# The last two eighths of both MLPs taken by halves of the tokens, with VectorE's queue pinned around them

## The chip, the cores and the metric

The program runs on one core of one Trainium2 chip. The metric is device time of one execution in microseconds (us); three runs of the kernel before took 1609.48, 1611.65 and 1611.97 us, so the median is 1611.65 us. TensorE (PE in the profile) multiplies matrices into PSUM, VectorE (DVE) and ScalarE (ACT) work on SBUF and PSUM, GpSimd (POOL) on SBUF, and SyncE (SP) issues the transfers. Each of these queues runs its instructions in order.

## The reference

Two transformer blocks on 512 tokens of width 1024. Both end in an MLP with a squared ReLU:

```python
# first block
h = rms_norm(x, norm_mlp[l])
x = x + jnp.square(jax.nn.relu(h @ w_up[l])) @ w_down[l]
return rms_norm(x, norm_final)
# second block
n2 = rms_norm_2(h, norm_mlp_pre[l])
hid = jnp.square(jax.nn.relu(jnp.einsum('bsd,df->bsf', n2, w_up[l])))
mlp_out = jnp.einsum('bsf,fd->bsd', hid, w_down[l])
h = h + rms_norm_2(mlp_out, norm_mlp_post[l])
```

The hidden width is 4096. What comes before the MLPs (block attention and gated linear attention, cross attention, the gated MLP of the second block and its dilated attention) is not touched.

## The kernel before

Products are made to float32 accuracy from three passes: each operand is split into a high part (ScalarE copies it to the narrower format) and a low part (VectorE subtracts the high part from the source). `split` (L316, L317) does this for activations, `load` (L247 to L249) for weights: a transfer into a staging tile `st` (three buffers), the copy on ScalarE, the subtraction on VectorE, after which the staging tile is free for a later transfer. `mm3` (L304) issues the three matmuls.

`mlp` holds the hidden layer as eight eighths `r[0]` to `r[7]`, each of 512 hidden columns by 512 tokens. `up(m)` makes 128 of those columns in a PSUM bank of the `tr` pool (two banks), and `evac` takes it out with a ReLU on ScalarE (L1033) and a square on GpSimd (L1034). The first six eighths go down in three rounds `g` of seven products `i`, in sums and differences of halves, as in Strassen's scheme. A product accumulates in two PSUM banks, one for each `c` in 0 and 1, and `fold` adds a bank to the output on VectorE (L1085) when the product is done. Products 0, 3, 5 and 6 share the banks named x: product 6 goes on accumulating in the bank that product 5 left, so its first matmul for a `c` has to wait until `fold` of product 5 has read that bank. After each product stands one `up`, after the seventh two.

The last two eighths, `e` = 6 and 7, go down plainly: for each token chunk `c` of 128 tokens and each half `b` of the output columns one bank with twelve matmuls (a unit, below). Eighth 6 goes first, `b` by `b`; then eighth 7, `c` by `c`, and `done(c, b)` starts what follows a finished chunk. In the first MLP that is `norm2` (L943 to L967: norms of the chunk on ScalarE, GpSimd and VectorE, then eight transposes on TensorE and the splits into `ah` and `al`); the second block's first products (`heads_qk` by `fm_halves`, tokens 0 to 255 first, then 256 to 511) wait for it. In the second MLP it is the final norm and the output.

The program's order on each queue comes from a scheduler that places each instruction where its own time model thinks it ready. Tile pools choose the buffer by the same model. `issue_after(ins)` queues what is traced inside it on the engine of `ins` behind `ins`, in order only.

Of the kernel before, what the change touches and what calls it, by code (L numbers as in the profile page):

```python
# [10 lines left out]
F32R = mybir.dt.float32r  # L11
# [9 lines left out]
P = 128  # L21
T = 512
D = 1024
KT = 8
NC = 4
# [85 lines left out]
class Kernel:  # L111
# [907 lines left out]
    def mlp(self, sfx, h, out, fresh, done):  # L1019

        nc, th = self.nc, self.th
        self.enter("pf" + sfx)
        key, up_key = f"w_down{sfx}", f"w_up{sfx}"
        r = {}

        def evac(m, ps):
            e = m // 4
            if m % 4 == 0:  # L1030
                r[e] = self.m8([P, 4, T], F32, "relu")
            t = r[e][:, m % 4, :]
            nc.scalar.activation(t, ps, AF.Relu)  # L1033
            nc.gpsimd.tensor_mul(t, t, t)  # L1034

        def up(m):
            (w,) = [self.weight(up_key, m, ahead=2)]
            ps = self.tr()
            for k in range(KT):
                self.mm3(ps, w[0][:, k, :], w[1][:, k, :], *self.a_all()(k), k == 0, k == KT - 1)  # L1040
            evac(m, ps)


        w = [self.weight(up_key, m, ahead=3) for m in range(4)]
        pss = [self.acc() for _ in range(4)]
        for hf in range(2):
            yield [h[2 * hf], h[2 * hf + 1]]
            s = slice(256 * hf, 256 * hf + 256)
            for i, p in enumerate(pss):
                for k in range(KT):  # L1050
                    self.mm3(p[:, s], w[i][0][:, k, :], w[i][1][:, k, :], *self.a_all(s)(k), k == 0, k == KT - 1)
                yield
        for m, ps in enumerate(pss):
            evac(m, ps)
        for m in range(4, 8):
            up(m)
            yield
        lo, hi = slice(0, 256), slice(256, 512)
        keep = {n: self.k4([P, 2, 512], F32, n) for n in ("p1", "p5", "u2")}
        sums = {}  # L1060

        def a_sum(g, i):

            a, b = r[2 * g], r[2 * g + 1]
            src = (a[:, :, lo], b[:, :, lo], None, None, None, a[:, :, lo], b[:, :, hi])[i]
            if i == 2:
                sums["t"] = src = self.ph.tile([P, 4, 256], F32, tag="asum", bufs=1, name=self.name("asum"))
                nc.gpsimd.tensor_add(src, a[:, :, hi], b[:, :, hi])
            elif i == 3:
                src = sums["t"]  # L1070
                nc.gpsimd.tensor_sub(src, src, a[:, :, lo])
            elif i == 4:
                src = sums["t"]
                nc.gpsimd.tensor_sub(src, b[:, :, lo], src)
            elif i == 5:
                nc.gpsimd.tensor_sub(src, src, a[:, :, hi])  # L1076
            t = self.m8([P, 2, 4, 256], F32R, "as")
            self.split(src, t[:, 0], t[:, 1])
            sums[g, i] = t

        def put(dst, ps, first):
            if first:
                nc.scalar.activation(dst, ps, AF.Copy)
            else:
                nc.vector.tensor_add(dst, dst, ps)  # L1085

        def fold(i, c, g):

            ps = sums["xyzxzxx"[i]][c]
            n = {0: "p1", 2: "p5", 3: "u2"}.get(i)  # L1090
            if n:
                put(keep[n][:, c, :], ps, g == 0)
            else:
                put(out(*{1: (c, 0), 4: (c, 1), 5: (2 + c, 1), 6: (2 + c, 0)}[i]), ps, g == 0 and fresh)

        for g in range(3):
            for i in range(7):
                for j in range(i, min(i + 3, 7)):
                    if (g, j) not in sums:
                        a_sum(g, j)  # L1100
                w = self.weight(key, g, i, ahead=2)
                ch = "xyzxzxx"[i]
                if i < 3:
                    sums[ch] = [(self.aux if i == 1 else self.acc)() for _ in range(2)]
                t = sums[g, i]
                for c in range(2):
                    for k in range(4):
                        wh, wl = (v[:, k % 2, :] for v in w[k // 2])
                        self.mm3(sums[ch][c], t[:, 0, k, self.cs(c)], t[:, 1, k, self.cs(c)], wh, wl,
                                 i < 3 and k == 0, k == 3, more=i >= 3)  # L1110
                    fold(i, c, g)
                    yield
                up(8 * g + 8 + i)
                yield
                if i == 6:
                    up(8 * g + 15)
                    yield
        for n, c0, b in (("p1", 0, 0), ("u2", 0, 1), ("p5", 2, 1)):
            for c in range(2):
                nc.gpsimd.tensor_add(out(c0 + c, b), out(c0 + c, b), keep[n][:, c, :])  # L1120

        for e in (6, 7):
            hl = [self.m8([P, 4, T], F32R, "hid") for _ in range(2)]
            for k in range(4):
                self.split(r[e][:, k, :], hl[0][:, k, :], hl[1][:, k, :])
            w = [None, None]
            for c, b in [(c, b) for c in range(NC) for b in range(2)] if e == 7 else [(c, b) for b in range(2) for c in range(NC)]:
                if c == 0:
                    w[b] = self.weight(key, 8 * b + e)
                ps = self.acc()  # L1130
                self.tm(ps, lambda k: (hl[0][:, k, self.cs(c)], hl[1][:, k, self.cs(c)]), [w[b]])
                put(out(c, b), ps, False)
                if e == 7:
                    done(c, b)
                yield


    def block2_mix(self):
# [492 lines left out]
```

## Time and profile before

| | us |
|---|---|
| median of three runs | 1611.65 |
| the profiled execution | 1610.89 |
| its span in the trace | 1609.1 |
| TensorE busy with matmuls | 1580.2 |
| VectorE, ScalarE, GpSimd busy | 971.2, 686.6, 531.0 |

The profiled execution is 0.76 us below the median. The span is what the trace covers; the remaining 1.8 us lie around it. Times in the trace count from the span's start. A row of the timeline has its start, how long it lasted, the engine, the line, the operation, what it writes and reads, its shape, a count when equal rows were merged, and in brackets the idle time of the engine before it with what ended that.

### The profile page before, as it was taken

To read this page: it belongs to the slowest core of one execution; us is meant where nothing else is said; L and a number is where in the kernel's file an instruction comes from. 1 tells how busy PE (TensorE), PEld (TensorE's weight loads), DVE (VectorE), ACT (ScalarE), POOL (GpSimd) and SP (SyncE) were. 2 spreads that over 40 slices of the span, in tenths; PEclk is the share of its full clock that TensorE was granted. 3 is DMA by queue.
4 is the path that set the end of the run, shared out by engine and by line. 5 is a ranking of instruction groups with operands and counts; after the bars stand their busy time and mean duration, and the time that the engine had idled before them with its cause. 6 is when DMAs were issued, how large, how long until landed. Compare 5 with 4: busy or idle time off the path is not lost.

```text
span 1609.1 us, 21890 instructions
## 1 busy us (share of the span) xinstructions
PE 1580.2 (98%) x8930; PEld 1342.8 (83%) x8930; DVE 971.2 (60%) x1195; ACT 686.6 (43%) x1053; POOL 531.0 (33%) x360
## 2 busy tenths in 40 slices
PE   9999999999999999999999999999999999999987
PEld 8777878898898888887799899888888988888876
DVE  5566575554657868686644554464245567686844
ACT  6455464343444534344523333374323445353431
POOL 1121220000017474762250532330021274756621
PEclk9999999999999999999999999999999999999999
DMA  8404223421341323223403302322424523232221
GB/s 289 157 28 138 90 75 114 156 79 53 98 157 61 132 91 118 90 82 133 140 27 136 101 21 86 105 79 85 164 80 157 191 71 131 90 119 81 88 94 66
DMA packets 50437, 171.08 MB, mean 106 GB/s; under 512 B 6208, under 2 KB 6992, under 8 KB 50336
## 3 DMA queue, kind: packets, MB, share of 16 engines
q1 hardware_dynamic: 50336, 169.68, 31.2%
q8 instruction: 70, 1.15, 0.3%
q14 instruction: 31, 0.25, 0.0%
HBM read 163.35 MB, written 8.93 MB: 107 GB/s over the span
## 4 chain that ended last, share of the span: by engine, by line
PE 44%; POOL 2%; DVE 2%; issue 1%; ACT 1%; DMA 0%; POOLq 0%; DVEq 0%; ACTq 0%
PE acc L304 34%; PE tr L304 7%; PE aux L304 2%; POOL raw L289 1%; PE tr L313 1%; DVE acc L1085 0%; DMA st<-in_w_down 0%; DVE as L317 0%; DVE acc L1507 0%; ACT junk L1495 0%; DVE wlo L249 0%; DVE wt L317 0%; POOL relu L1076 0%; DVE wu L249 0%; POOL relu L1034 0%
## 5 line engine op out<-in xcount | busy, mean ns | idle before, releaser
L304 PE MATMUL tr<-ah,wu 128*128 128x512 f32 x896 | 283.1, 389 | 0.0
L249 DVE TENSOR_TENSOR wlo<-st,whi 128x1024 fp32r<-128x1024 f32 (+3 forms) x159 | 200.6, 1286 | 125.0 <-ACT whi L248 100.2
L248 ACT ACTIVATE whi<-st 128x1024 fp32r<-128x1024 f32 (+3 forms) x159 | 160.9, 1039 | 196.9 <-PE acc L304 113.2
L304 PE MATMUL acc<-ah,whi 128*128 128x512 f32 (+1 forms) x576 | 213.1, 372 | 0.8 <-ACT ah L316 0.8
L304 PE MATMUL acc<-wt,as 128*128 128x512 f32 x864 | 205.3, 393 | 8.4 <-DVE acc L1085 4.8
L304 PE MATMUL acc<-al,whi 128*128 128x512 f32 (+1 forms) x576 | 212.2, 369 | 0.6 <-DVE al L317 0.6
L304 PE MATMUL acc<-ah,wlo 128*128 128x512 f32 (+1 forms) x576 | 211.6, 368 | 0.0
L317 DVE TENSOR_TENSOR wt<-raw,wt 128x1024 fp32r<-128x1024 f32 x84 | 169.8, 2036 | 54.8 <-ACT wt L316 47.0
L304 PEld LDWEIGHTS acc<-wt,as 128*128 128x128 f32 x864 | 164.1, 190 | 43.5 <-DVE acc L1085 5.2
L304 PEld LDWEIGHTS tr<-ah,wu 128*128 128x128 f32 x896 | 168.3, 188 | 35.0
L304 PE MATMUL tr<-al,wu 128*128 128x512 f32 x448 | 174.3, 389 | 0.0
L1034 POOL TENSOR_TENSOR relu<-relu 128x512 f32<-128x512 f32 x64 | 94.1, 1472 | 209.7 <-ACT relu L1033 182.9
L289 POOL TENSOR_TENSOR raw<-raw,raw 128x1024 f32<-128x1024 f32 x48 | 153.7, 3217 | 14.4 <-DMA raw<-in_w_down 9.6
L304 PE MATMUL acc<-whi,ah 128*128 128x512 f32 (+2 forms) x432 | 146.5, 346 | 1.4 <-ACT ah L434 1.4
L304 PE MATMUL acc<-wlo,ah 128*128 128x512 f32 (+2 forms) x432 | 146.1, 342 | 0.0
L304 PE MATMUL acc<-whi,al 128*128 128x512 f32 (+2 forms) x432 | 144.2, 342 | 0.0
L316 ACT ACTIVATE wt<-raw 128x1024 fp32r<-128x1024 f32 x84 | 87.9, 1055 | 89.0 <-POOL raw L289 58.7
L304 PEld LDWEIGHTS acc<-ah,whi 128*128 128x128 f32 x576 | 108.9, 190 | 19.7 <-issue 1.7
L304 PEld LDWEIGHTS acc<-ah,wlo 128*128 128x128 f32 x576 | 109.4, 190 | 17.8
L304 PEld LDWEIGHTS acc<-al,whi 128*128 128x128 f32 x576 | 109.5, 190 | 17.6 <-DVE al L317 0.8
L249 DVE TENSOR_TENSOR wu<-st,wu 128x1024 fp32r<-128x1024 f32 x64 | 107.7, 1690 | 25.2 <-ACT wu L248 25.2
L304 PEld LDWEIGHTS tr<-al,wu 128*128 128x128 f32 x448 | 84.1, 188 | 17.4
(344 smaller groups left out, 2801.8 us busy)
## 6 DMA issues: line engine op xcount, KB each, us to landing
st<-in_w_up SPq DMA_DIRECT2D x64, 512.0 KB, 4.2
raw<-in_w_down SPq DMA_DIRECT2D x48, 512.0 KB, 4.7
st<-in_w_in_2f SPq DMA_DIRECT2D x44, 512.0 KB, 4.3
st<-in_w_in_u SPq DMA_DIRECT2D x20, 512.0 KB, 5.1
st<-in_w_out SPq DMA_DIRECT2D x16, 512.0 KB, 4.3
st<-in_w_down SPq DMA_DIRECT2D x16, 512.0 KB, 3.8
st<-in_w_xk SPq DMA_DIRECT2D x8, 512.0 KB, 4.5
st<-in_w_xv SPq DMA_DIRECT2D x8, 512.0 KB, 4.0
```

What stands on the lines that cost most here:

```text
L248: nc.scalar.activation(hi[:, s, :], st, AF.Copy)
L249: nc.vector.tensor_sub(lo[:, s, :], st, f32(hi[:, s, :]))
L289: nc.gpsimd.tensor_sub(r[name][:, s, :], r[x][:, s, :], r[y][:, s, :])
L304: self.nc.tensor.matmul(ps, lhsT, rhs, start=start, stop=stop, skip_group_check=more)
L313: self.nc.tensor.transpose(ps, src, self.ident)
L316: self.nc.scalar.activation(hi, src, AF.Copy)
L317: self.nc.vector.tensor_sub(lo, src, f32(hi))
L1034: nc.gpsimd.tensor_mul(t, t, t)
```

## The change

`fold` keeps the instruction that adds the fifth-index product's last bank (`i == 5`, `c == 1`) to the output. In the third round, the weight that product 6 asks for ahead of its use and the last `up` are queued on VectorE behind that addition, and so are the splits of the operands of eighths 6 and 7. The sixteen units of those eighths are reordered: first eighth 6 with `b` = 0 for all four chunks (the first two of these in the `aux` banks instead of `acc`), then what is left of chunks 0 and 1, then what is left of chunks 2 and 3. So the new list goes by halves of the tokens.

```diff
-                nc.vector.tensor_add(dst, dst, ps)
+                self.folded = nc.vector.tensor_add(dst, dst, ps).ins
...
-                w = self.weight(key, g, i, ahead=2)
+                late = g == 2 and i == 6
+
+                with self.tc.issue_after(folded) if late else ExitStack():
+                    w = self.weight(key, g, i, ahead=2)
...
+                    if i == 5:
+                        folded = self.folded
...
-                    up(8 * g + 15)
+                    with self.tc.issue_after(folded) if late else ExitStack():
+                        up(8 * g + 15)
...
-        for e in (6, 7):
-            hl = [self.m8([P, 4, T], F32R, "hid") for _ in range(2)]
-            for k in range(4):
-                self.split(r[e][:, k, :], hl[0][:, k, :], hl[1][:, k, :])
-            w = [None, None]
-            for c, b in [(c, b) for c in range(NC) for b in range(2)] if e == 7 else [(c, b) for b in range(2) for c in range(NC)]:
...
+        hl, w = {}, {}
+        units = [(6, 0, c) for c in range(NC)]
+        units += [(e, b, c) for e, b in ((6, 1), (7, 0), (7, 1)) for c in range(2)]
+        units += [(6, 1, c) for c in (2, 3)] + [(7, b, c) for c in (2, 3) for b in range(2)]
+        for n, (e, b, c) in enumerate(units):
+            if e not in hl:
+                hl[e] = [self.m8([P, 4, T], F32R, "hid") for _ in range(2)]
+                with self.tc.issue_after(folded):
+                    for k in range(4):
+                        self.split(r[e][:, k, :], hl[e][0][:, k, :], hl[e][1][:, k, :])
...
+            ps = (self.aux if n < 2 else self.acc)()
```

Three places show how the queues move. The first is VectorE at the end of the third round in the first MLP. `x_3230` and `x_3232` are the output chunks 2 and 3, `acc_6048` and `acc_6049` the x banks for `c` = 0 and 1, `hid_6572` the low part of eighth 6, `wu_6460` the weight of the last `up`, `wlo_6492` and `wlo_6529` the down weights of eighth 6. Before:

```order
L249 TENSOR_TENSOR wu_6460<-st_6461,wu_6460 128x1024
L1085 TENSOR_TENSOR x_3226<-x_3226,acc_6196 128x512
L1085 TENSOR_TENSOR x_3228<-x_3228,acc_6197 128x512
L249 TENSOR_TENSOR wlo_6492<-st_6493,whi_6491 128x1024
L249 TENSOR_TENSOR wlo_6492<-st_6497,whi_6491 128x1024
L1085 TENSOR_TENSOR x_3230<-x_3230,acc_6048 128x512
L317 TENSOR_TENSOR hid_6572<-relu_6106,hid_6571 128x512 x2
L249 TENSOR_TENSOR wlo_6529<-st_6530,whi_6528 128x1024
L249 TENSOR_TENSOR wlo_6529<-st_6534,whi_6528 128x1024
L317 TENSOR_TENSOR hid_6572<-relu_6106,hid_6571 128x512 x2
L1085 TENSOR_TENSOR x_3232<-x_3232,acc_6049 128x512
```

The same place of the changed kernel:

```order
L1085 TENSOR_TENSOR x_3226<-x_3226,acc_6196 128x512
L1085 TENSOR_TENSOR x_3228<-x_3228,acc_6197 128x512
L249 TENSOR_TENSOR wlo_6492<-st_6493,whi_6491 128x1024
L249 TENSOR_TENSOR wlo_6492<-st_6497,whi_6491 128x1024
L1085 TENSOR_TENSOR x_3230<-x_3230,acc_6048 128x512
L1085 TENSOR_TENSOR x_3232<-x_3232,acc_6049 128x512
L249 TENSOR_TENSOR wu_6460<-st_6461,wu_6460 128x1024
L249 TENSOR_TENSOR wlo_6529<-st_6530,whi_6528 128x1024
L249 TENSOR_TENSOR wlo_6529<-st_6534,whi_6528 128x1024
L317 TENSOR_TENSOR hid_6572<-relu_6106,hid_6571 128x512 x4
```

The addition to `x_3232` has moved from behind six instructions to directly behind the one to `x_3230`; `wu_6460`, ahead of all of them before, now stands behind both. The second MLP shows the same two lists with other numbers.

The second place is ScalarE there; `relu_6391<-tr_6433` empties the bank that the last `up` will write. Before:

```order
L248 ACTIVATE whi_6528<-st_6530 128x1024
L248 ACTIVATE whi_6528<-st_6534 128x1024
L316 ACTIVATE hid_6571<-relu_6106 128x512 x4
L248 ACTIVATE whi_6637<-st_6639 128x1024
L316 ACTIVATE hid_6703<-relu_6391 128x512
L248 ACTIVATE whi_6637<-st_6643 128x1024
L1033 ACTIVATE relu_6391<-tr_6433 128x512
```

And in the changed kernel:

```order
L248 ACTIVATE whi_6528<-st_6530 128x1024
L316 ACTIVATE hid_6571<-relu_6106 128x512 x4
L248 ACTIVATE whi_6528<-st_6534 128x1024
L316 ACTIVATE hid_6675<-relu_6391 128x512
L248 ACTIVATE whi_6637<-st_6639 128x1024
L1033 ACTIVATE relu_6391<-tr_6433 128x512
```

One copy of a weight less stands ahead of that ReLU. In the changed kernel the staging tile of `st_6639` is the one that `wu_6460` frees; before, it was one that `wlo_6492` frees.

The third place is VectorE at the end of the first MLP; `v_...` are the chunks in `norm2` (L950 starts one, L963 ends it), `wlo_6969` a weight of the second block. Before:

```order
L1085 TENSOR_TENSOR x_3226<-x_3226,acc_6751 128x512
L950 TENSOR_TENSOR v_939_6765<-x_3226,gain_6737 128x1024
L1085 TENSOR_TENSOR x_3228<-x_3228,acc_6782 128x512
L963 SCALAR_TENSOR_TENSOR v_939_6765<-v_939_6765,r_943_6774,gain_6739 128x1024
L1085 TENSOR_TENSOR x_3228<-x_3228,acc_6796 128x512
L950 TENSOR_TENSOR v_946_6810<-x_3228,gain_6737 128x1024
L1085 TENSOR_TENSOR x_3230<-x_3230,acc_6827 128x512
```

And in the changed kernel:

```order
L1085 TENSOR_TENSOR x_3226<-x_3226,acc_6737 128x512
L950 TENSOR_TENSOR v_938_6751<-x_3226,gain_6709 128x1024
L1085 TENSOR_TENSOR x_3228<-x_3228,acc_6768 128x512
L950 TENSOR_TENSOR v_944_6782<-x_3228,gain_6709 128x1024
L963 SCALAR_TENSOR_TENSOR v_938_6751<-v_938_6751,r_942_6760,gain_6711 128x1024
L1085 TENSOR_TENSOR x_3230<-x_3230,acc_6799 128x512
L963 SCALAR_TENSOR_TENSOR v_944_6782<-v_944_6782,r_948_6791,gain_6711 128x1024
L1085 TENSOR_TENSOR x_3232<-x_3232,acc_6813 128x512
L249 TENSOR_TENSOR wlo_6969<-st_6970,whi_6968 128x1024
```

Chunk 0 is finished after the ninth unit (it was the tenth) and chunk 1 after the tenth (it was the twelfth); chunks 2 and 3 are finished after the fourteenth and the sixteenth, as before. On TensorE the transposes of chunks 0 and 1 now stand inside the thirteenth and fourteenth unit (they stood inside the fourteenth and sixteenth), and the second block's first half follows the last unit without a break: 61 of its matmuls stand ahead of the transposes of chunk 2, and 27 more ahead of those of chunk 3.

## Rows read from the trace of the kernel before

**Rows 1.** The page, busy time of each engine, with its share and count.
```profile
PE 1580.2 (98%) x8930; PEld 1342.8 (83%) x8930; DVE 971.2 (60%) x1195; ACT 686.6 (43%) x1053; POOL 531.0 (33%) x360
```

**Rows 2.** Timeline of PE, first MLP, products 5 and 6 of the third round.
```profile
716.76 5.60 PE L304 MATMUL acc<-wt,as 128*128 128x512 f32 x24
722.20 0.39 PE L304 MATMUL tr<-ah,wu 128*128 128x512 f32 x1
...
727.64 2.88 PE L304 MATMUL acc<-wt,as 128*128 128x512 f32 x12
734.08 4.61 PE L304 MATMUL acc<-wt,as 128*128 128x512 f32 x12 [3.56 <-DVE x L1085]
738.52 0.40 PE L304 MATMUL tr<-ah,wu 128*128 128x512 f32 x1
```

**Rows 3.** Timeline of PE, second MLP, product 6 of the third round.
```profile
1533.28 2.88 PE L304 MATMUL acc<-wt,as 128*128 128x512 f32 x12
1540.95 4.44 PE L304 MATMUL acc<-wt,as 128*128 128x512 f32 x12 [4.80 <-DVE acc L1085]
1545.23 0.40 PE L304 MATMUL tr<-ah,wu 128*128 128x512 f32 x1
```

**Rows 4.** Windows: busy us (count) of PE, PEld, DVE, ACT, POOL; PEclk, DMA share, GB/s.
```profile
727.60:738.60 11.00, 7.44 (x26) 5.63 (x26) 9.72 (x11) 5.60 (x9) 4.50 (x2) 0.84 0.44 150
1533.20:1545.30 12.10, 7.30 (x27) 5.59 (x26) 9.57 (x11) 6.15 (x9) 4.32 (x2) 0.86 0.43 148
...
795.00:803.20 8.20, 5.50 (x30) 5.09 (x31) 7.44 (x10) 6.91 (x12) 4.03 (x9) 0.80 0.79 265
803.20:823.90 20.70, 20.70 (x179) 20.70 (x179) 6.30 (x12) 3.61 (x7) 6.16 (x8) 1.00 0.21 72
```

**Rows 5.** Timeline of DVE, first MLP, around product 6.
```profile
717.89 1.77 DVE L249 TENSOR_TENSOR wu<-st,wu 128x1024 fp32r<-128x1024 f32 x1 [0.21 <-ACT wu L248]
...
720.78 4.17 DVE L249 TENSOR_TENSOR wlo<-st,whi 128x1024 fp32r<-128x1024 f32 x2
724.87 0.67 DVE L1085 TENSOR_TENSOR x<-x,acc 128x512 f32<-128x512 f32 x1
728.66 1.29 DVE L317 TENSOR_TENSOR hid<-relu,hid 128x512 fp32r<-128x512 f32 x2 [3.11 <-ACT hid L316]
...
733.35 0.68 DVE L1085 TENSOR_TENSOR x<-x,acc 128x512 f32<-128x512 f32 x1
```

**Rows 6.** Timeline of DVE, second MLP, the addition for chunk 2.
```profile
1530.55 0.67 DVE L1085 TENSOR_TENSOR acc<-acc,acc 128x512 f32<-128x512 f32 x1
```

**Rows 7.** Timeline of ACT, first MLP, the ReLU of the bank.
```profile
735.83 0.58 ACT L1033 ACTIVATE relu<-tr 128x512 f32<-128x512 f32 x1
```

**Rows 8.** Issues of down weights on SP: count, size, us to landing.
```profile
st<-in_w_down SPq DMA_DIRECT2D x16, 512.0 KB, 3.8
```

**Rows 9.** Timeline of PE from the first unit into the second block.
```profile
749.42 0.39 PE L304 MATMUL acc<-whi,hid 128*128 128x512 f32 x1
...
787.28 0.60 PE L313 MATMUL tr<-ident,v 128*128 128x128 f32 x4
...
788.07 0.71 PE L304 MATMUL acc<-whi,hid 128*128 128x512 f32 x2
...
795.71 0.74 PE L304 MATMUL acc<-ah,whi 128*128 128x256 f32 x4 [0.81 <-ACT ah L316]
797.87 0.63 PE L313 MATMUL tr<-ident,v 128*128 128x128 f32 x4 [1.42 <-DVE v L963]
...
799.51 0.39 PE L304 MATMUL acc<-al,whi 128*128 128x256 f32 x1 [0.58 <-DVE al L317]
...
823.98 0.40 PE L304 MATMUL acc<-ah,whi 128*128 128x512 f32 x1
```

**Rows 10.** Timeline of DVE, chunk 3: its last addition, and the end of norm2.
```profile
795.00 0.68 DVE L1085 TENSOR_TENSOR x<-x,acc 128x512 f32<-128x512 f32 x1
...
804.12 1.28 DVE L963 SCALAR_TENSOR_TENSOR v<-v,r,gain 128x1024 f32<-128x1024 f32 x1 [0.60 <-POOL r L958]
```

More of the change, by code (lines that the diff above doesn't have):

```diff
@@ L1120, in mlp @@
                 nc.gpsimd.tensor_add(out(c0 + c, b), out(c0 + c, b), keep[n][:, c, :])
-        for e in (6, 7):
-            hl = [self.m8([P, 4, T], F32R, "hid") for _ in range(2)]
-            for k in range(4):
-                self.split(r[e][:, k, :], hl[0][:, k, :], hl[1][:, k, :])
-            w = [None, None]
-            for c, b in [(c, b) for c in range(NC) for b in range(2)] if e == 7 else [(c, b) for b in range(2) for c in range(NC)]:
[L1128 to L1135, printed above, removed]
+        hl, w = {}, {}
[8 more added lines that the diff above has]
+                        self.split(r[e][:, k, :], hl[e][0][:, k, :], hl[e][1][:, k, :])
+            if (e, b) not in w:
+                w[e, b] = self.weight(key, 8 * b + e)
+            ps = (self.aux if n < 2 else self.acc)()
+            self.tm(ps, lambda k: (hl[e][0][:, k, self.cs(c)], hl[e][1][:, k, self.cs(c)]), [w[e, b]])
+            put(out(c, b), ps, False)
+            if e == 7:
+                done(c, b)
+            yield
     def block2_mix(self):
```

## The prediction

> **What bounds the kernel now.** I read the engines' busy time first: TensorE is busy for 1580.2 of 1609.1 us [rows 1], so time can only come from the 29 us in which it is not, and from stretches in which its clock is low. VectorE is busy for 60% and no bound by itself; what counts is what stands ahead of what in its queue.
>
> TensorE's timeline next, at the two places that the change touches. In an undisturbed product 24 matmuls of 512 columns take 722.20 - 716.76 = 5.44 us, or 0.227 us each [rows 2]. Product 6 of the first MLP's third round starts at 727.64, does twelve, waits 3.56 us for VectorE's addition to x, and is done at 738.52: 10.88 us, so it loses 10.88 - 5.44 = 5.44 us [rows 2]. In the second MLP the same product runs from 1533.28 to 1545.23, 11.95 us with a wait of 4.80, and loses 6.51 us [rows 3]. In both the loss is larger than the wait, because the twelve matmuls behind it are slow: the granted clock is 0.84 and 0.86 of full over these stretches [rows 4], that is, partly at 1.2 GHz instead of 2.4.
>
> The third place is the passage into the second block, from the first unit at 749.42 to the first 512-column matmul behind the halves at 823.98: 74.56 us [rows 9]. Its work is 16 units of twelve at 0.227 = 43.5; four times eight transposes at 788.07 - 787.28 = 0.79, so 3.2; and 192 matmuls of 256 columns, at half of 0.227 21.8, or at the 20.70 / 179 = 0.116 of the window behind 803 [rows 4] 22.2. That is 68.5 to 68.9, so 5.7 to 6.1 us are lost. 0.81 + 1.42 + 0.58 = 2.8 of them are waits for chunks 1 and 2 [rows 9]; the rest is again low clock, 0.80 granted from 795 to 803.2 [rows 4].
>
> **The change part by part.** *The addition moves up.* VectorE adds chunk 2 (x bank of c = 0) at 724.87 and chunk 3 (c = 1) only at 733.35 [rows 5], though product 5 left that bank at 722.20 [rows 2]. In between it waited 3.11 us for ScalarE's copies of eighth 6, which stand behind a weight's transfer, and did four splits and two weight parts. In the changed order the addition follows directly: 724.87 + 0.61 to 726.2. TensorE needs the bank at 727.64 + 2.72 = 730.36. That is 4 us to spare, so the wait of 3.56 goes and with it the slow matmuls: 5.44 us. In the second MLP chunk 2 is added at 1530.55 [rows 6], so chunk 3 is done by 1531.9, and TensorE needs it at 1533.28 + 2.72 = 1536.0: 6.51 us go.
>
> What is late next? `wu_6460`, the weight of the last `up`, goes from 717.89 (1.77 us [rows 5]) to behind both additions, so it is ready at about 728.2 (2.1 us, the mean of the two at 720.78, when GpSimd works beside it). The last `up` starts at 727.64 + 2 x 5.44 = 738.52: 10 us to spare. Its staging tile comes free 8 us later, and the transfer behind it, a part of eighth 7's weight, is issued at 728.2 instead of when the second part of `wlo_6492` ended, at 724.9 [rows 5]. It lands 3.8 us later by the median [rows 8], at 732.0; ScalarE's copy takes 1.0 and its ReLU out of the bank of the last `up` follows, done at 733.7, where it started at 735.83 before [rows 7]. TensorE wants that bank at 738.52: nearly 5 us to spare. The splits of eighth 6, 0.65 us each, move behind the weight parts, from 728.66 on [rows 5] to about 732 to 735. Their reader is the first unit, now due at 738.52 + 5.44 = 743.96: 9 us. All this is hidden by the two `up`s, 10.88 us of TensorE; without them the splits would show with up to 3 us.
>
> *The units by halves.* No matmul is added or removed. Chunk 0 is finished one unit (2.72 us) earlier, chunk 1 two units (5.44). So chunks 0 and 1 need not be ready until the last unit is done, and the first half of the tokens' matmuls covers chunks 2 and 3. The old waits of 0.81 and 0.58 us, for chunk 1, have 5.4 us more; that of 1.42, for chunk 2's `norm2` ahead of its transposes, has 61 matmuls, 6.9 us, more. Chunk 3 is the tight one: its last addition started at 795.00 and its `norm2` ended at 804.12 + 1.28, 10.4 us later [rows 10], with weight parts and splits between. In the new order 88 matmuls of 0.113 and eight transposes, 10.8 us, lie ahead of it. A chain as slow as before just fits. From both sides: this passage gives back between 0, if chunk 3 now waits for what chunk 2 waited for, and all of 5.9. I take 4.9, near the upper end, because every wait that the rows show has over 5 us of new cover, and charge 1.0 for chunk 3.
>
> *The banks.* The first two units use the `aux` pair, idle since product 1, instead of the z pair, which was free too; nothing waits for either. The weight of eighth 6 for b = 1 is held until the twelfth unit (it was the eighth), 10.9 us longer, so one weight of the second block loads that much later. It is first used behind the 192 matmuls, 22 us after the last unit. I cost it at 0; if that cover were gone it would be 10.9.
>
> *The tail.* Chunk 3 is still the last in the second MLP, with both its units at the end: 0.
>
> The sum: 5.44 + 6.51 + 4.9 = 16.85 us off the profiled execution's 1610.89 gives 1594.0. The median of the runs is 0.76 above that execution, so 1594.8.
>
> **The clock, by rows and by the skill.** The rows show the granted clock below full in the three stretches that hold waits, and 1.00 behind the last one [rows 4]. The Trainium skill, "TensorE: Matmul & The Clock Gate", section "What's actually happening", says that the half rate is the default state and that activity releases it. By that rule the slow matmuls are the waits' own cost and go with them, which the sum assumes. If they did not depend on the waits, the gain would be the waits alone, the second rival below.
>
> **Rivals.**
> 1. *The passage keeps its loss*: chunk 2 or 3 is late for its transposes. For it: the 10.4 against 10.8 us, and the transfers there, at 265 GB/s [rows 4]. Against: VectorE has less queued ahead of chunk 3, as the splits of chunks 0 and 1 come earlier. Only 11.95 go: 1610.89 - 11.95 + 0.76 = 1599.7.
> 2. *The clock falls anyway*, for the mix of work there: only the waits go, 3.56 + 4.80 + 2.8 = 11.2, so 1600.5. For it: in the passage the clock stays low after the waits have ended. Against: the same kinds of matmul run at 1.00 from 803.2 on.
> 3. *The last `up` becomes the stall, and the kernel is slower.* The copy of eighth 7's weight stands ahead of the ReLU that frees the bank, and its transfer now waits for `wu_6460`. Landing after 738.52 - 1.6 = 736.9, it stalls TensorE; to eat 16.85 us in two MLPs it must stall 8.4 us in each, so land after 745.3, 17 us after issue. Each us beyond costs 2 us: 1613 at 18 us. Against: a median landing of 3.8 [rows 8].
> 4. *The additions do not come earlier*, because what holds VectorE is ahead of both: no change, 1611.7. Against: chunk 2's addition came at 724.87, in time.
>
> **How the numbers follow.** Forecast 0.74, at 1594.8, with its own range of 1591 (the whole 5.9, and runs 2 us lower, as the lowest before was) to 1598. Rivals 1 and 2 together 0.17, at 1599 to 1601; a milder form of 3, one stall of 3 to 6 us, 0.03, at 1598 to 1602; rival 4 0.03; rival 3 0.03. So 1590.5 to 1601.5 holds eight in ten. Within 0.2% (3.2 us, about what a measurement of this kernel can tell from no change) lie rival 4 and little else: faster 0.94, same 0.03, slower 0.03.
>
> **What would show it.** In the profile after, product 6 of both third rounds takes 5.44 us without a wait for VectorE, and the granted clock there is 1.00. From the first unit to the 512-column matmuls of the second block it is 69 to 70 us. The ReLU that frees the last `up`'s bank comes before it, and the tail from the last matmul to the end is unchanged. A wait at the transposes of chunk 2 or 3 is rival 1; a low clock without a wait rival 2; a wait of the last `up` for ScalarE rival 3. Any of these by more than 3 us makes the forecast wrong.

## The result and the profile after

The changed kernel takes 1592.7 us (median of four runs, 1589.91 to 1599.22), the kernel before 1610.57 on the same chip: a ratio of 0.9893, 95% interval 0.9872 to 0.9914. The profiled execution took 1594.01 us (before 1610.89), its span is 1592.2 us (before 1609.1).

The page of the changed kernel, busy time of each engine; it answers to [rows 1].

```profile
PE 1575.6 (99%) x8930; PEld 1340.8 (84%) x8930; DVE 971.4 (61%) x1195; ACT 686.0 (43%) x1053; POOL 532.9 (33%) x360
```

The same 8930 matmuls are 4.6 us less busy, and TensorE's time without work fell from 28.9 to 16.6 us. The busy times of the other engines moved by less than 2 us. TensorE's timeline of the changed kernel, product 6 of both third rounds and the first unit behind each, and then the second MLP's first unit in the kernel before, where [rows 3] do not reach; it answers to [rows 2, 3]:

```profile
727.77 5.60 PE L304 MATMUL acc<-wt,as 128*128 128x512 f32 x24
733.21 0.39 PE L304 MATMUL tr<-ah,wu 128*128 128x512 f32 x1
...
744.09 0.39 PE L304 MATMUL aux<-whi,hid 128*128 128x512 f32 x1
...
1523.44 5.60 PE L304 MATMUL acc<-wt,as 128*128 128x512 f32 x24
...
1539.76 0.39 PE L304 MATMUL aux<-whi,hid 128*128 128x512 f32 x1
```

```profile
1556.13 0.39 PE L304 MATMUL acc<-whi,hid 128*128 128x512 f32 x1
```

The 24 matmuls are one group again, without a wait in brackets: 733.21 - 727.77 = 5.44 us. The first unit comes 16.32 us behind the start of product 6 in both MLPs; before it was 21.78 (749.42 - 727.64 [rows 2, 9]) and 22.85 us (1556.13 - 1533.28 [rows 3]). So 5.46 and 6.53 us are back.

VectorE there, first MLP, answering to [rows 5]:

```profile
723.91 1.28 DVE L1085 TENSOR_TENSOR x<-x,acc 128x512 f32<-128x512 f32 x2
725.11 2.13 DVE L249 TENSOR_TENSOR wu<-st,wu 128x1024 fp32r<-128x1024 f32 x1
727.16 3.45 DVE L249 TENSOR_TENSOR wlo<-st,whi 128x1024 fp32r<-128x1024 f32 x2
730.53 2.48 DVE L317 TENSOR_TENSOR hid<-relu,hid 128x512 fp32r<-128x512 f32 x4
```

Both additions stand together and are done at 725.2; TensorE needs the second bank at 727.77 + 2.72 = 730.49. The weight of the last `up` and the splits follow. ScalarE behind that, answering to [rows 7]:

```profile
730.99 1.06 ACT L248 ACTIVATE whi<-st 128x1024 fp32r<-128x1024 f32 x1 [1.25 <-DMA st<-in_w_down]
731.96 0.58 ACT L1033 ACTIVATE relu<-tr 128x512 f32<-128x512 f32 x1
```

The copy still waits for its transfer, but the ReLU behind it ends at 732.5, and the last `up` wants that bank at 733.21 + 5.44 = 738.65.

The passage, TensorE: the first 256-column matmul, the last transposes of chunks 2 and 3, and the first 512-column matmul of the second block; it answers to [rows 9].

```profile
789.40 0.28 PE L304 MATMUL acc<-ah,whi 128*128 128x256 f32 x1
...
796.59 0.60 PE L313 MATMUL tr<-ident,v 128*128 128x128 f32 x4
...
800.64 0.60 PE L313 MATMUL tr<-ident,v 128*128 128x128 f32 x4
...
813.33 0.40 PE L304 MATMUL acc<-ah,whi 128*128 128x512 f32 x1
```

No row of it has a wait. It takes 813.33 - 744.09 = 69.24 us, where it took 74.56 [rows 9]: 5.32 us back. Chunk 3 on VectorE, its last addition and the end of `norm2`, answering to [rows 10]:

```profile
790.17 0.68 DVE L1085 TENSOR_TENSOR x<-x,acc 128x512 f32<-128x512 f32 x1
...
798.80 1.28 DVE L963 SCALAR_TENSOR_TENSOR v<-v,r,gain 128x1024 f32<-128x1024 f32 x1 [1.42 <-POOL r L958]
```

The chain ends at 800.08, 9.9 us after that addition's start and 0.56 us before TensorE takes it up at 800.64. Windows of the stretches that answer to [rows 4], with the same columns:

```profile
727.77:738.70 10.93, 10.93 (x50) 9.05 (x49) 10.93 (x13) 6.16 (x8) 1.93 (x2) 1.00 0.59 200
1523.40:1528.90 5.50, 5.50 (x26) 4.53 (x26) 5.45 (x7) 3.87 (x6) 1.16 (x2) 1.00 0.82 248
789.40:801.40 12.00, 12.00 (x104) 12.00 (x103) 9.77 (x10) 7.80 (x12) 4.82 (x8) 1.00 0.78 268
```

The granted clock, 0.80 to 0.86 before, is 1.00 (2.4 GHz) in all three, though transfers run there at 200 to 268 GB/s, no less than the 148 to 265 before.

### The profile page after: what moved, and what is told of

The parts are those of the page before. It is cut to its first block, busy times and chain, and to the rows that moved or that the text cites. A ratio compares the mean times of both kernels' runs of the same rounds, so it can differ in the third digit from the quotient of the medians.

```text
span 1592.2 us, 21897 instructions
## 1 busy us (share of the span) xinstructions
PE 1575.6 (99%) x8930; PEld 1340.8 (84%) x8930; DVE 971.4 (61%) x1195; ACT 686.0 (43%) x1053; POOL 532.9 (33%) x360
## 4 chain that ended last, share of the span: by engine, by line
PE 94%; DVE 2%; DMA 1%; ACT 1%; issue 1%; POOL 0%; SPq 0%; DVEq 0%; POOLq 0%; ACTq 0%
PE acc L304 63%; PE tr L304 20%; PE aux L304 8%; PE tr L313 2%; DMA st<-in_w_in_u 1%; DMA st<-in_w_up 0%; PE aux L313 0%; DVE wlo L249 0%; DMA xT<-in_x_T 0%; DVE glev L710 0%; ACT junk L331 0%; DVE acc L1519 0%; ACT whi L248 0%; ACT junk L1507 0%; DVE acc L1085 0%
## 5 line engine op out<-in xcount | busy, mean ns | idle before, releaser
L304 PE MATMUL acc<-wt,as 128*128 128x512 f32 x864 | 201.7, 389 | 0.0
L304 PEld LDWEIGHTS acc<-al,whi 128*128 128x128 f32 x576 | 108.7, 189 | 16.9 <-issue 0.6
```

The lines of the kernel that those rows point to most:

```text
L304: self.nc.tensor.matmul(ps, lhsT, rhs, start=start, stop=stop, skip_group_check=more)
```

## The experiments

Ratios are to the kernel before, run on the same chip, with 95% intervals.

**1. The pins alone.** The units of the kernel before, in the `acc` banks, with all three `issue_after`:

```
-        units = [(6, 0, c) for c in range(NC)]
...
+            with self.tc.issue_after(folded):
...
+            for c, b in [(c, b) for c in range(NC) for b in range(2)] if e == 7 else [(c, b) for b in range(2) for c in range(NC)]:
...
+                ps = self.acc()
...
```

> The three pins on VectorE stay, the sixteen units go back to the old list and to the acc banks. Theory (the pins remove the two stalls of product 6, the new list of units removes the losses in the passage, and the two do not touch each other): product 6 of both third rounds takes 5.44 us without a wait, which gives back 5.44 + 6.51 = 11.95 us, and the passage from the first unit to the 512-column matmul keeps its 74.6 us with its three waits of 0.6 to 1.4 us. Profiled 1610.9 - 11.95 = 1598.9 us, 0.9926 of the kernel before. Rival (the gain of the passage comes from the pins too, since the splits and weights behind them shift VectorE's queue): the passage falls towards 69 us here as well and the time towards 1594. Rival (the gain of product 6 needs the new list): no change, 1610.9.

1598.93 us, 0.9929 (0.9913 to 0.9944); profiled 1599.34. Its product 6 of the first MLP, the ends of its passage and the waits in it, on TensorE:

```profile
728.09 5.60 PE L304 MATMUL acc<-wt,as 128*128 128x512 f32 x24
...
744.41 0.39 PE L304 MATMUL acc<-whi,hid 128*128 128x512 f32 x1
...
790.70 0.74 PE L304 MATMUL acc<-ah,whi 128*128 128x256 f32 x4 [0.82 <-ACT ah L316]
...
792.84 0.63 PE L313 MATMUL tr<-ident,v 128*128 128x128 f32 x4 [1.40 <-DVE v L963]
...
794.49 0.38 PE L304 MATMUL acc<-al,whi 128*128 128x256 f32 x1 [0.58 <-DVE al L317]
...
818.97 0.40 PE L304 MATMUL acc<-ah,whi 128*128 128x512 f32 x1
```

Product 6 is whole, in the second MLP too (1528.27, 24 matmuls in one group), and the three waits of [rows 9] are there to 0.02 us. The passage, 744.41 to 818.97, takes 74.56 us, exactly as before. Both rivals fall: the pins do nothing to the passage, and product 6 does not need the new list.

**2. The list of units alone.** All pins gone, new list and banks kept:

```
-                late = g == 2 and i == 6
+                late = False
...
-                with self.tc.issue_after(folded):
+                with ExitStack():
```

> The new list of units with its aux banks stays, all three pins are gone; chunk 3's addition stands behind two weight parts and four splits again, as before. Theory: product 6 of the first MLP again waits 3.6 us for VectorE and takes 10.9 us at a granted clock near 0.85, that of the second MLP waits 4.8 and takes 12 us; the passage takes 69.2 us as in the changed kernel (74.6 before). Profiled 1610.9 - 5.3 = 1605.6 us, 0.9967 of before. Rival (the passage's gain comes from the pins): the passage keeps 74 us, 1610.9. If the two parts are independent, the gains of this run and of the run with the pins alone add up to the 16.9 us of the whole change; if they overlap, the sum is larger than that.

1605.64 us, 0.9972 (0.9958 to 0.9987); profiled 1605.60. TensorE, product 6 of the first MLP, then the ends of the passage:

```profile
728.46 2.88 PE L304 MATMUL acc<-wt,as 128*128 128x512 f32 x12
734.73 4.34 PE L304 MATMUL acc<-wt,as 128*128 128x512 f32 x12 [3.38 <-DVE x L1085]
...
749.80 0.39 PE L304 MATMUL aux<-whi,hid 128*128 128x512 f32 x1
...
819.03 0.40 PE L304 MATMUL acc<-ah,whi 128*128 128x512 f32 x1
```

The stall is back (3.38 us here, 4.82 in the second MLP), and the passage takes 819.03 - 749.80 = 69.23 us. So the two parts are independent: either alone does in its own stretch what it does in the whole change, and leaves the other's as it was. The profiled gains, 11.55 and 5.29 us, add up to 16.84, where the whole change gained 16.88. That they agree to 0.04 us is luck: four executions of the changed kernel alone lie up to 9 us apart.

**3. All units in the `acc` banks.**

```
-            ps = (self.aux if n < 2 else self.acc)()
+            ps = self.acc()
```

> The changed kernel with all sixteen units in the acc banks: the first two take the z pair instead of the aux pair. Theory (the z pair is free by then, so the choice of banks is worth nothing): within 0.3 us of the changed kernel in the profile, 1594.0, 0.9893 of before. Rival (the z pair is still being added up by VectorE, whose queue is now fuller ahead of it): the first unit waits for VectorE, 0.6 to 3 us in each MLP, so 1595 to 1600.

1592.50 us, 0.9889 (0.9875 to 0.9903), profiled 1592.16: nothing that the times can tell from the changed kernel, and no wait at the first unit. The profiled execution is 1.85 us under that of the changed kernel, more than the 0.3 us expected, but 1.06 us of that stand ahead of product 6 (it starts at 726.71, not 727.77), before the edit can act. The other banks are worth nothing that could be measured.

**4. Only the splits pinned.**

```
-                late = g == 2 and i == 6
+                late = False
```

> The changed kernel without two of its three pins: only the splits of eighths 6 and 7 stay behind the addition; the weight of the last up goes ahead of the additions again, and the second part-pair of eighth 6's weight between the additions of chunks 2 and 3. Theory (it was the splits, which wait for ScalarE's copies, that held the addition up; the weights only take VectorE's time): chunk 3's addition comes after two weight parts, 2.1 + 1.2 us behind the one of chunk 2, near 729.3 to 729.9 in the first MLP, where TensorE needs it at 730.5: no wait or one under 0.5 us in each MLP, and 1594 to 1595.5 us. Rival (all three pins are needed): product 6 waits 1 to 3 us in each MLP and its matmuls are slow behind the wait, 1598 to 1604.

1593.02 us, 0.9895 (0.9877 to 0.9914). TensorE, product 6 of the second MLP, and VectorE ahead of the addition it waits for:

```profile
1521.24 2.88 PE L304 MATMUL acc<-wt,as 128*128 128x512 f32 x12
1524.72 3.02 PE L304 MATMUL acc<-wt,as 128*128 128x512 f32 x12 [0.60 <-DVE acc L1085]
```

```profile
1522.85 1.23 DVE L249 TENSOR_TENSOR wlo<-st,whi 128x1024 fp32r<-128x1024 f32 x1 [2.29 <-ACT whi L248]
1523.99 0.68 DVE L1085 TENSOR_TENSOR acc<-acc,acc 128x512 f32<-128x512 f32 x1
```

No wait that a row marks in the first MLP, 0.60 us in the second, a little over what was expected. Mainly the splits held the addition up; the other two pins buy slack, 5 us in the first MLP in place of none. The weight parts do not only take VectorE's time, as the theory has it: one of them, between the two additions, waited 2.29 us for ScalarE's copy, more than the 0.60 us that is left of the stall.

**5. The wait removed from TensorE's side.** The kernel before, unpinned, with one `up` of the third round ahead of product 6 (and its weight earlier in the order of loads); its lines below are four higher, L1089 is L1085:

```
...
+                if (g, i) != (2, 6):
+                    up(8 * g + 8 + i)
+                    yield
+                if (g, i) == (2, 5):
+                    up(30)
+                    yield
```

> The kernel before, with no pin and the old list of units; only in the third round one of the two ups that followed product 6 goes ahead of it, in both MLPs. VectorE's queue stays as it was: chunk 3's addition starts at 733.35 in the first MLP, behind the splits that wait for ScalarE. But product 6 starts 5.44 us later, at 733.1, and needs the bank at 735.8. Theory (what cost the time is TensorE's wait, and the slow matmuls come with it, whatever removes it): no wait in the first MLP, none or under 0.5 us in the second, product 6 takes 5.44 us at a granted clock of 1.00 in both, so 11.95 us go: 1610.9 - 11.95 = 1598.9, 0.9926, with VectorE idle in the same place as before. Rival (the clock falls there for the mix of work, and the pins prevented that): only the waits go, 3.56 + 4.80 = 8.4 us, 1602.5, and the granted clock of product 6 stays near 0.85. Rival (it is the early addition itself that counts, since other work hangs on it): no change, 1610.9.

1598.76 us, 0.9929 (0.9917 to 0.9942). VectorE around chunk 3's addition in the first MLP, then TensorE's product 6 in both:

```profile
728.93 1.29 DVE L321 TENSOR_TENSOR hid<-relu,hid 128x512 fp32r<-128x512 f32 x2 [3.33 <-ACT hid L320]
...
733.62 0.68 DVE L1089 TENSOR_TENSOR x<-x,acc 128x512 f32<-128x512 f32 x1
```

```profile
733.75 5.60 PE L308 MATMUL acc<-wt,as 128*128 128x512 f32 x24
...
1533.93 5.60 PE L308 MATMUL acc<-wt,as 128*128 128x512 f32 x24
```

VectorE waits for the splits as in [rows 5] and adds as late, but TensorE comes later still. The granted clock is 1.00 over product 6 in both MLPs (windows 733.75:739.19 and 1533.93:1539.37), without any pin: the low clock went with the wait, whatever removed it. It is another way to the same 12 us.

**6. A wait put back, in four doses.** The changed kernel with n subtractions ahead of chunk 3's addition in the first MLP and m in the second; TensorE's order is held:

```
...
+                    behind = ExitStack()
+                    if g == 2 and i == 5 and c == 1:
+                        d = self.folded
+                        for _ in range(7 if up_key == "w_up" else 9):
+                            with self.tc.issue_after(d):
+                                d = nc.vector.tensor_sub(sums["t"][:, 0:2, :], r[6][:, 0, :], r[6][:, 1, :]).ins
+                        behind = self.tc.issue_after(d)
+                    with behind:
+                        fold(i, c, g)
...
```

With 7 and 9:

> The changed kernel with a chosen wait put back. Between the additions of chunks 2 and 3 VectorE does subtractions of 128x512 into a scratch tile that nothing reads, 7 in the first MLP and 9 in the second; the weight of the last up goes ahead of the additions, and TensorE's order is held as it is in the changed kernel. At 1.06 us each beside GpSimd and 0.62 alone this should make product 6 wait 1.3 us in the first MLP and 2.6 in the second. Known so far: a wait of 0.60 us cost 0.14 us beyond itself in the matmuls behind it, waits of 3.38 to 4.82 cost 1.5 to 1.9 us beyond. Theory (the clock falls with the wait once that is long enough, by an amount that does not grow with it): the loss beyond the wait is either near 0.1 or near 1.7 us in each of the two, and the step lies between 0.6 and 3.4. Rival (the loss beyond the wait grows with its length): 0.5 to 0.7 us behind 1.3, 1.1 to 1.3 behind 2.6. In all 1594 + 4 to 7 us.

1602.58 us, 0.9948 (0.9933 to 0.9963), 1.6 us over the expected range; the profiled execution, 1599.98, lies inside it. Its waits were 0.56 and 0.74 us longer than worked out. TensorE, product 6's second half in both MLPs:

```profile
731.27 4.62 PE L304 MATMUL acc<-wt,as 128*128 128x512 f32 x12 [1.86 <-DVE x L1085]
...
1531.90 3.02 PE L304 MATMUL acc<-wt,as 128*128 128x512 f32 x12 [3.34 <-DVE acc L1085]
```

The shorter wait brought the clock down (granted 0.63 over the twelve matmuls), the longer one did not (1.00). Neither theory had that, so the kernel ran once more:

> The same kernel as e6_dose once more, for its profile alone. There the first MLP's product 6 waited 1.86 us and its twelve matmuls behind took 4.62 us at a granted clock of 0.63, while the second MLP's waited 3.34 us and its matmuls took 3.02 at 1.00. Theory (whether the clock falls behind a wait of this size is not set by the wait's length, and differs from one execution to the next): the waits are the same within 0.1 us, and at least one of the two places comes out the other way. Rival (it is set by the place: what runs on the other engines, or how long TensorE had been busy before): the same picture, 4.62 and 3.02 us.

Its same two rows:

```profile
732.33 3.01 PE L304 MATMUL acc<-wt,as 128*128 128x512 f32 x12 [1.86 <-DVE x L1085]
...
1530.87 4.51 PE L304 MATMUL acc<-wt,as 128*128 128x512 f32 x12 [3.35 <-DVE acc L1085]
```

Both places came out the other way, with waits equal to 0.01 us. The counts were then swapped, and set to 11 and 12:

> The kernel of e6_dose with the two counts swapped, 9 subtractions in the first MLP and 7 in the second: waits near 3.1 and 2.1 us instead of 1.86 and 3.34. Theory (chance): each place may come out with or without slow matmuls (4.4 to 4.7 us for twelve, or 3.0). Rival (set by the length, the longer of the two being the harmless one): slow behind the second MLP's wait, full speed behind the first's. Rival (set by the place): slow behind the first MLP's, full speed behind the second's.

> The kernel of e6_dose with 11 and 12 subtractions: waits near 4.3 and 5.2 us. All four waits of 3.38 to 4.82 us in the kernel before and in the one with the new list of units alone were followed by slow matmuls, 4.34 to 4.61 us for twelve. Theory (a long wait always brings the clock down, a short one by chance): slow behind both, 4.3 to 4.7 us. Rival (chance at any length): full speed behind one of them at least, 3.0 us.

One execution each, 1604.86 and 1612.35 us (the kernel before, also once, 1609.81). The rows of the swapped kernel, then of the long one:

```profile
738.15 4.47 PE L304 MATMUL acc<-wt,as 128*128 128x512 f32 x12 [3.36 <-DVE x L1085]
...
1536.70 3.02 PE L304 MATMUL acc<-wt,as 128*128 128x512 f32 x12 [1.91 <-DVE acc L1085]
```

```profile
737.87 4.91 PE L304 MATMUL acc<-wt,as 128*128 128x512 f32 x12 [5.51 <-DVE x L1085]
...
1541.64 5.49 PE L304 MATMUL acc<-wt,as 128*128 128x512 f32 x12 [6.24 <-DVE acc L1085]
```

The long kernel's waits are longer than expected, and both are followed by slow matmuls, as its theory has it, 4.91 and 5.49 us for twelve where 4.3 to 4.7 were expected. Waits at product 6 in all profiles together: slow matmuls did not follow the one of 0.60, followed one of three of 1.86 to 1.91, three of four of 3.34 to 3.38, and all five of 3.56 to 6.24 us. "Set by the place" and "the longer is the harmless one" fall. With so few cases the five of five do not show that a long wait always brings the clock down.

**7. Chunk 3's chain made longer**, in the changed kernel (its L964 is L963):

```
-        nc.vector.tensor_mul(v, x, g1)
+        for _ in range(3 if c == 3 else 1):
+            nc.vector.tensor_mul(v, x, g1)
```

> The changed kernel with chunk 3's first multiplication of norm2 done three times instead of once (the same result, 2 x 1.28 us more in its chain). In the changed kernel that chain ended 0.56 us before TensorE wanted it. Theory (the passage's gain hangs on chunk 3's chain, with half a us to spare): TensorE waits 2 to 3 us ahead of the transposes of chunk 3, some slow matmuls follow, the passage takes 71.5 to 74 us instead of 69.2, and the time is 1596 to 1599. Rival (the chain has more cover than the rows show, because VectorE's own queue sets it): no wait over 0.5 us, 1594. Rival 1 of the forecast would have looked like this run.

1595.26 us, 0.9915 (0.9892 to 0.9938). The profiled execution, 1593.95, reached the first unit 2.4 us earlier than that of the changed kernel. TensorE in the passage:

```profile
741.72 0.39 PE L304 MATMUL aux<-whi,hid 128*128 128x512 f32 x1
...
801.49 0.63 PE L313 MATMUL tr<-ident,v 128*128 128x128 f32 x4 [2.12 <-DVE v L964]
802.80 0.72 PE L304 MATMUL acc<-ah,whi 128*128 128x256 f32 x4 [0.25 <-ACT ah L316]
...
814.06 0.40 PE L304 MATMUL acc<-ah,whi 128*128 128x512 f32 x1
```

A wait of 2.12 us and a small one behind it, 72.34 us for the passage instead of 69.24. The slow matmuls that the theory expected did not come, nor its 1596 to 1599 us: the granted clock is 1.00 over the whole passage. So the new list lives on half a us at chunk 3, and rival 1 would have looked like this. The times alone can't tell this run from the changed kernel.

**8. The tail.** The last chunk's first multiplication behind its last addition:

```
-            nc.vector.tensor_mul(u[:, s], u[:, s], gs[0][:, s])
+            for h in {(3, 0): (), (3, 1): (0, 512)}.get((c, b), (512 * b,)):
+                with self.tc.issue_after(self.folded):
+                    nc.vector.tensor_mul(u[:, h : h + 512], u[:, h : h + 512], gs[0][:, h : h + 512])
```

> The changed kernel with one more reordering, at its very end: the multiplication by the final gain for the last chunk's first half is queued behind the addition of its second half, which it held up by 0.9 us (that addition started at 1584.54, while TensorE's last matmul had ended at 1583.45). Theory (the tail is a chain that starts with that addition): from the last matmul's start to the span's end it takes 8.2 to 8.5 us instead of 9.1, which the profile shows and the times can hardly tell: 1593.1, 0.9888. Rival (the multiplications then stand on the chain themselves, two in a row behind it): 9.1 to 9.8 us.

1594.19 us, 0.9894 (0.9877 to 0.9911). The profiled execution, 1598.25, was 5.9 us late at the first unit already, long before the edit: over the first 245 us the granted clock was 0.95 in it, 0.97 in that of the changed kernel and 0.99 in that of experiment 7, which came early. Its last matmul starts at 1588.35 of a span of 1596.5: the tail is 8.15 us, just under the 8.2 to 8.5 expected, where it was 1592.2 - 1583.06 = 9.14 in the changed kernel. One us is gained in the trace, and none that the times can show.

## Why the prediction was right, step by step

- *The addition moves up* (5.44 + 6.51 = 11.95 us): 5.46 and 6.53 in the trace of the whole change, 11.55 between the profiled executions of experiment 1 and of the kernel before. The mechanism is shown from two sides, by the pins and by experiment 5. Of the pins that on the splits did nearly all of it; without the others 0.60 us of wait was left.
- *What is late next*: the weight of the last `up` ready at 727.24 (said 728.2), the transfer behind it landed by 730.99 (732.0), the ReLU done at 732.5 (733.7), the splits at 733.0 (732 to 735). All hidden, as said; rival 3 never came near. The additions were done at 725.2, not 726.2, because that weight no longer stands ahead of them: 1 us that the working had overlooked.
- *The units by halves* was the term that was mis-sized: 4.9 us forecast, 5.32 measured, and 5.33 in experiment 2. The 1.0 charged for chunk 3 was too much, since TensorE waits nowhere in the passage. That its chain fits is partly luck: the working let the 10.4 us chain and the 10.8 us of cover start together. In the trace the cover starts at 789.40, with the last unit's end, and the addition only at 790.17, 0.77 us later, which alone would have used up the 0.4 to spare. The chain then took 9.9 us and not 10.4, and the cover, with the 256-column matmuls at 0.118 us and not 0.113, 800.64 - 789.40 = 11.24 and not 10.8; so 0.56 was left. Experiment 7 shows that chunk 3 is where a loss would come first.
- *Banks*: 0, experiment 3. *Tail*: 1592.2 - 1583.06 = 9.14 us, where it was 1609.1 - 1599.42 = 9.68, so 0.54 less and not 0. It comes with the list: with the pins alone the tail is 9.72, with the list alone 9.13.
- *The sum*: the forecast of 1594.8 is 2.1 us above the measured median of 1592.7, inside its own range. That it meets the profiled execution to 0.01 us (1594.0 and 1594.01) is luck, as the executions lie between 1589.91 and 1599.22; and the 0.76 us that was added for the median has no counterpart, since over four runs each the medians lie 0.3 us (before) and 1.3 us (after) under the profiled executions. The sum was also closer than its parts. They come to 5.46 + 5.32 + 6.53 + 0.54 = 17.85 us; stretches that the change does not touch ran 0.94 us longer (0.13 ahead of product 6, 0.81 between the passage and the second MLP's product 6), which leaves the 16.9 of the spans. The 16.85 of the forecast had neither.
- *Rival 2*, the clock falling anyway: refuted by the 1.00 in the three stretches once their waits are gone, and by experiment 5. But the reason given was too simple. It took the slow matmuls as a fixed price of the waits; with 5.44 - 3.56 and 6.51 - 4.80 that is 1.9 and 1.7 us. Experiment 6 shows that for waits of 1.9 to 3.4 us the price is paid in some executions and not in others. The waits of 3.56 and 4.80 us lay where it was always paid here, so the sum held.

## What to carry to other kernels

Where an accumulating product must wait for another engine to read its bank, look at what stands ahead of that read in the reader's queue: work that itself waits for a third engine can hold the read up by far more than its own length (3.1 us of waiting for two splits of 0.65 here), and either moving it behind the read or giving TensorE other work first removed the stall whole. Test the parts of a change alone, and compare the stretch that each is meant for: here each part kept its gain alone, and two of three pins and the choice of banks were worth nothing that the times could show. Price a TensorE wait with its clock, but as a chance: at product 6 a wait of 1.9 to 3.4 us cost either 0.1 or some 1.5 to 1.7 us beyond itself.

## What was not expected of the hardware

The same program, with the same wait to 0.01 us, was followed by twelve matmuls at full clock in one execution and at a granted 0.63 or 0.64 in the other. Windows over the twelve matmuls behind the wait, first MLP then second, in the second run of experiment 6 (columns as in [rows 4]):

```profile
732.30:735.40 3.10, 3.07 (x13) 2.55 (x14) 3.10 (x2) 0.00 (x0) 3.04 (x2) 1.00 0.22 62
1530.80:1535.40 4.60, 4.54 (x13) 3.65 (x14) 4.60 (x4) 0.30 (x1) 4.17 (x2) 0.64 0.50 155
```

In the first run it was 0.63 and 1.00 in the same two places. Behind the longest wait, 6.24 us, the granted clock was 0.50 (1.2 GHz) over all twelve. The first run's first MLP, then the long kernel's second MLP:

```profile
731.30:735.90 4.60, 4.60 (x13) 3.63 (x14) 4.60 (x3) 0.40 (x1) 4.17 (x2) 0.63 0.38 123
1541.60:1547.10 5.50, 5.46 (x13) 4.31 (x14) 5.50 (x6) 0.64 (x1) 2.19 (x1) 0.50 0.49 171
```

The Trainium skill, "TensorE: Matmul & The Clock Gate", section "What's actually happening", says that the monitor behind the clock runs freely, not in step with the program, and that the count of slow matmuls at a kernel's start therefore differs between runs of one kernel. The rows agree as far as they go, and show it in the middle of a kernel: what differs between the two executions is not the wait. That it is the monitor's phase no run here shows.

The 192 matmuls of 256 columns in the passage ran at two paces with the clock at 1.00: 0.118 us each up to about 800 and 0.113 behind in the changed kernel, 0.113 first and 0.118 later in the kernel before. If all 192 ran at the one pace or the other, that would be 0.9 us, by an estimate from these two paces; the cause stays open.
